# RWKV recurrence: one solve of four tiles against two half chains of two tiles that take turns on TensorE

## The chip, the core and the metric

One NeuronCore of a Trainium2 chip runs the whole program in one launch. The metric is device time in microseconds. The kernel before took 2664.04 us, the median of three runs (2661.07 to 2665.22).

## What is computed

Two layers of a decoder trunk over 256 tokens of width 2048. Layer 0 is latent attention beside a gated delta rule; layer 1 is RWKV-7 time mixing; each is followed by a SwiGLU feed-forward block, and all of it is in float32. The change touches only the RWKV layer:

```
r, k, v = xr @ w_r, xk @ w_k, xv @ w_v          # three 2048 x 2048 projections
def step(state, inp):                            # 32 heads of 64
    r_t, d_t, k_t, v_t, kk_t, a_t = inp
    sk = einsum("bhvk,bhk->bhv", state, kk_t)
    state = state*d_t - sk*(kk_t*a_t) + v_t*k_t
    return state, einsum("bhvk,bhk->bhv", state, r_t)
y = group_norm(y)*ln_w + ln_b + bonus;  return (y * gate) @ w_o
```

The kernel does not walk the tokens. It cuts them into four chunks of 64, inverts one triangular 64x64 matrix per head and chunk, and walks the four chunks.

## The kernel before, in words

**Tiles.** 2048 channels are 16 tiles of 128 partitions, two heads to a tile. Tiles come in 8 pairs. Per pair, `rec_pre` makes r and k: 192 matmuls of 256 columns (lines L317, L319, L320, since every product is done in three parts, high by high, high by low, low by high). `rec_head` makes from them the four matrices `KR`, `AB`, `KG`, `BT` of each tile and the values `V`, with matmuls into the PSUM tag `ph` (L1364, L1374, L1394).

**The solve.** `rec_solve(g)` takes four tiles, and there are four of them, g = 0 to 3. It has three parts:
- *Doubling*: four levels of two steps. A step is one burst `mul` of 64 products of 32x32 (128 matmul instructions, since a float32 product is two passes) at L1413, whose result goes through PSUM to VectorE (`W`, L1427) or to ScalarE and VectorE (`Tm`, L1431, and the transposed `Rc`, L1432), and from there into the next burst. Two smaller bursts (L1439, L1450) end it.
- *Scan*: four chunks. In each, `X` (L1466, L1469), `E` (L1476) and the state `S` (L1488, L1490), each waiting for the one before to come back from PSUM.
- *Output*: for each pair of the four tiles, 88 products (L1509), a sum over the head (`headsum`), the norm, the gate (L1531), and the result goes to DRAM or into `xs_hi`, `xs_lo`.

Each step of a solve needs the result of the step before, so a solve by itself leaves TensorE waiting. The waiting time is meant to be filled by projections: `rec_pre` of later pairs, and in the last two solves `wo_part` (matmuls of 512 columns, L317, L322, L323). I call these two "projections" below, whatever their width.

**Buffers.** `NH` = 5 tiles of `KR`, `AB`, `KG`, `V`, `BT` exist, so that beside the four of a running solve one more can be made; the other three wait for the solve's output. The tag `gt` holds one gate, `BK` one scaled k tile of a head.

**What sets the order.** `weave` emits the tasks by hand-written due times (`LS` is the time given to a solve). A scheduler with a timeline of its own then sets the order of each engine's instructions; on the chip each engine runs its queue in that order. SP issues the loads.

Of the kernel before, what the change touches and what calls it, by code (L numbers as in the profile page):

```python
# [19 lines left out]
P = 128  # L20
# [24 lines left out]
def constants():  # L45
# [32 lines left out]
    out["cent"] = np.tile(np.eye(64) - 1.0 / 64, (2, 1))  # L78
# [25 lines left out]
def tile_trunk(ctx: ExitStack, tc: tile.TileContext, A, out, dbg=None):  # L104
# [1156 lines left out]
    rebank(2, {"ph": 3, "pc": 3})  # L1261
    rcx, rcp = phase("rec")
    RB = {"r_t": 2, "KR": NH, "AB": NH, "KG": NH, "V": NH, "BT": NH, "bon": 3, "pd": 2}
# [13 lines left out]
    def c64(ap):  # L1277
        return ap.rearrange("p (c n) -> p c n", n=64)
# [32 lines left out]
    def rec_head(pr2):  # L1311
# [77 lines left out]
        vb = c64(pbank("ph"))  # L1389
        for j in range(2):  # L1390
            for ch in range(4):
                tsl = slice(ch * 64, ch * 64 + 64)
                for s_ in HS:
                    mm(vb[s_, 4 * j + ch, :], lhsT=vc[s_, j, tsl], rhs=C("cent")[s_], start=True, stop=True)  # L1394
        for j, c in enumerate(cs):
            V = Sr([P, 4, 64], "V")
            act(V, vb[:, 4 * j : 4 * j + 4, :], AF.Copy)
            heads[c] = (*out[j], V)
        heads["pair", pr2] = pd, bon

    def rec_solve(g):
# [3 lines left out]
        U4 = range(4)  # L1405
        UC = [(u, ch) for u in U4 for ch in range(4)]

        def mul(L, X):

            v_ = c32(pbank("pc"))  # L1410
            for u, ch in UC:
                for b, s_ in enumerate(QS):
                    mm(v_[s_, 4 * u + ch, :], lhsT=L(b, u, ch), rhs=X[s_, 4 * u + ch, :], start=True, stop=True)  # L1413
            return v_


        Rw = Sr([P, 16, 64], "R")
        for u in U4:
            tt(Rw[:, 4 * u : 4 * u + 4, :], AB[u][:, :, 0:64], bcn("rm1t", 4), ALU.mult)
        R = Sr([P, 16, 32], "Rc")  # L1420
        tt(R, Rw[:, :, 0:32], Rw[:, :, 32:64], ALU.add)
        Tm = Sr([P, 16, 32], "Tm")
        nc.vector.transpose(flat(Tm), flat(R))
        for lv in (2, 4, 8, 16):
            W = Sr([P, 16, 32], "W")
            p_ = mul(lambda b, u, ch: AB[u][QS[b], ch, 32 * (b % 2) : 32 * (b % 2) + 32], Tm)
            tt(W, p_, bcn(f"rl{lv}", 16), ALU.mult)  # L1427
            yield 1
            p_ = mul(lambda b, u, ch: R[QS[b], 4 * u + ch, :], W)
            Tm, R = Sr([P, 16, 32], "Tm"), Sr([P, 16, 32], "Rc")  # L1430
            act(flat(Tm), flat(p_), AF.Copy)  # L1431
            nc.vector.transpose(flat(R), flat(p_))  # L1432
            yield 1

        Rc, R = R, Sr([P, 16, 64], "R")
        p_ = c32(pbank("pc"))
        for u, ch in UC:
            for b in (0, 2):
                mm(p_[QS[b + 1], 4 * u + ch, :], lhsT=AB[u][QS[b], ch, 32:64], rhs=Tm[QS[b], 4 * u + ch, :],  # L1439
                   start=True, stop=True)  # L1440
        W = Sr([P, 16, 32], "W")
        act(W[QS[1]], p_[QS[1]], AF.Copy)
        nc.vector.tensor_copy(W[QS[3]], p_[QS[3]])
        tt(R.rearrange("p c (b n) -> p c b n", b=2), Rc.unsqueeze(2).to_broadcast([P, 16, 2, 32]),
           C("bd32").rearrange("p (b n) -> p b n", b=2).unsqueeze(1).to_broadcast([P, 16, 2, 32]), ALU.mult)
        yield 1
        p_ = c32(pbank("pc"))
        for u, ch in UC:
            for b in (0, 2):
                mm(p_[QS[b], 4 * u + ch, :], lhsT=W[QS[b + 1], 4 * u + ch, :], rhs=Rc[QS[b + 1], 4 * u + ch, :],  # L1450
                   start=True, stop=True)
        act(R[QS[0], :, 32:64], p_[QS[0]], AF.Copy)
        nc.vector.tensor_copy(R[QS[2], :, 32:64], p_[QS[2]])
        yield 1

        Ss = Sr([P, 3, 4, 64], "S")
        E2 = [Sr([P, 2, 4, 64], t) for t in ("Tm", "Rc")]

        def E(ch):
            return E2[ch // 2][:, ch % 2]  # L1460

        for ch in range(4):
            px = c64(pbank("pc")[:, :T])
            for u in U4:
                for s_ in HS:
                    mm(px[s_, u, :], lhsT=KG[u][s_, ch, 0:64], rhs=V[u][s_, ch, :], start=True, stop=ch == 0)  # L1466
                if ch:
                    for s_ in HS:
                        mm(px[s_, u, :], lhsT=KR[u][s_, ch, 0:64], rhs=Ss[s_, ch - 1, u, :], start=False, stop=True)  # L1469
            X = Sr([P, 4, 64], "X")  # L1470
            act(X, px, AF.Copy)
            yield 1
            pe = c64(pbank("pc")[:, :T])
            for u in U4:
                for s_ in HS:
                    mm(pe[s_, u, :], lhsT=R[s_, 4 * u + ch, :], rhs=X[s_, u, :], start=True, stop=True)  # L1476
            nc.vector.tensor_copy(E(ch), pe)
            if ch in (1, 2):
                dec = Sr([P, 4, 64], "X")
                for u in range(2):  # L1480
                    tt(dec[:, 2 * u : 2 * u + 2, :], Ss[:, ch - 1, 2 * u : 2 * u + 2, :],
                       pds[u][:, :, ch].unsqueeze(2).to_broadcast([P, 2, 64]), ALU.mult)
            yield 1
            if ch < 3:
                pS = c64(pbank("pc")[:, :T])
                for u in U4:
                    for s_ in HS:
                        mm(pS[s_, u, :], lhsT=BT[u][s_, ch, 1, :], rhs=V[u][s_, ch, :], start=True, stop=False)  # L1488
                    for s_ in HS:
                        mm(pS[s_, u, :], lhsT=BT[u][s_, ch, 0, :], rhs=E(ch)[s_, u, :], start=False, stop=True)  # L1490
                if ch:
                    tt(Ss[:, ch], dec, pS, ALU.add)
                else:
                    nc.vector.tensor_copy(Ss[:, 0], pS)
                yield 1
        for v in range(2):
            pr2 = 2 * g + v
            py = pbank("pc")
            y4 = py.rearrange("p (u c n) -> p u c n", u=2, n=64)
            for w_ in range(2):  # L1500
                u = 2 * v + w_
                for i in range(3):
                    for ch in range(4):
                        if i == 1 and ch == 0:
                            continue
                        for s_ in HS:
                            lhs, rhs = ((V[u][s_, ch, :], KG), (Ss[s_, max(ch - 1, 0), u, :], KR),
                                        (E(ch)[s_, u, :], AB))[i]
                            mm(y4[s_, w_, ch, :], lhsT=lhs, rhs=rhs[u][s_, ch, 64:128], start=i + ch == 0, stop=i == 2,  # L1509
                               skip_group_check=True)  # L1510
            yield 1
            sq = Sr([P, 2, T], "W")
            act(flat(sq), py, AF.Square)
            pv = pbank("pc")
            hl = Sr([P, 2, 2 * T], "R", F32R)
            headsum(pv, flat(sq), hl[:, 0, :], hl[:, 1, :])
# [128 lines left out]
```

## Time and profile before

| | us |
|---|---|
| median of three runs | 2664.04 |
| the profiled execution | 2662.39 |
| its span | 2660.6 |
| PE busy in the span | 2569.1 (97%) |
| DVE busy | 1540.4 (58%) |
| ACT busy | 1315.0 (49%) |

The RWKV recurrence stands between 1395 and 1908 us. "Busy" counts a matmul from its start to its modelled end, and those overlap, so a busy PE need not be at its peak: in the solves the number of matmuls in a stretch tells more than the share. PEclk in the tables is the granted clock of TensorE; 1.00 is its upper level of 2.4 GHz, 0.50 its lower one of 1.2 GHz.

### The profile page before, as it was taken

The numbers are of one execution on the slowest core, as the hardware profiler recorded it, in microseconds if no ns is written. First come the engines' busy times: TensorE is split into PE (matmuls) and PEld (weight loads), VectorE is DVE, ScalarE is ACT, GpSimd is POOL, SyncE is SP. The second block draws the span as 40 slices with busy tenths as digits, with TensorE's granted clock in tenths as the row PEclk, the third lists the DMA queues.
The fourth block names the chain that finished last, engine by engine and source line by source line (L and its number), as shares of the span: only waits on it lengthen the run. The fifth ranks groups of instructions, "written<-read, shape, count | busy, mean of one in ns | idle before, by whom it ended". The sixth has DMA issues, their size and how long they took to land.

```text
span 2660.6 us, 50321 instructions
## 1 busy us (share of the span) xinstructions
PE 2569.1 (97%) x21102; PEld 2225.8 (84%) x21102; DVE 1540.4 (58%) x2183; ACT 1315.0 (49%) x1953; POOL 33.3 (1%) x99
## 2 busy tenths in 40 slices
PE   8999999999999999998999998889899999999998
PEld 8999988788888888887999897777688888888886
DVE  7866666655444554458776574664655444555455
ACT  6665545544444434445577473553554444443443
POOL 1000000000000000000000000000000000000000
PEclk9999999999999999998999998899899999999999
DMA  7544546666566656655587442533366666666665
GB/s 208 148 121 129 175 144 198 179 185 194 183 192 187 193 187 190 190 186 176 177 278 219 130 133 67 171 99 126 112 185 190 190 192 193 187 193 194 190 184 164
DMA packets 275331, 461.49 MB, mean 173 GB/s; under 512 B 23752, under 2 KB 89216, under 8 KB 274336
## 3 DMA queue, kind: packets, MB, share of 16 engines
q1 hardware_dynamic: 274720, 458.12, 56.6%
q8 instruction: 165, 2.70, 0.4%
q14 instruction: 62, 0.51, 0.1%
q0 software_dynamic: 384, 0.16, 0.0%
HBM read 441.93 MB, written 16.29 MB: 172 GB/s over the span
## 4 chain that ended last, share of the span: by engine, by line
PE 92%; DVE 3%; ACT 2%; DMA 2%; issue 1%; SPq 0%; DVEq 0%; ACTq 0%
PE pw L317 27%; PE pw L322 20%; PE pw L323 20%; PE pw L320 7%; PE pw L319 7%; PE pc L1413 2%; PE ph L1364 1%; PE pc L1509 1%; DVE wlo L274 1%; DMA raw<-in_rwkv_w_o_dram 1%; PE pc L1476 1%; ACT whi L273 1%; PE pw L1176 1%; PE pc L1490 0%; PE pc L1469 0%
## 5 line engine op out<-in xcount | busy, mean ns | idle before, releaser
L274 DVE TENSOR_TENSOR wlo<-raw,whi 128x1024 fp32r<-128x1024 f32 (+1 forms) x814 | 975.9, 1201 | 881.1 <-ACT whi L273 877.4
L273 ACT ACTIVATE whi<-raw 128x1024 fp32r<-128x1024 f32 (+1 forms) x814 | 844.4, 1040 | 971.3 <-PE pw L323 795.9
L322 PE MATMUL pw<-wlo,xs_hi 128*128 128x512 f32 x1664 | 651.9, 392 | 0.0
L323 PE MATMUL pw<-whi,xs_lo 128*128 128x512 f32 x1664 | 648.8, 391 | 0.0
L317 PE MATMUL pw<-whi,xs_hi 128*128 128x512 f32 x1664 | 599.6, 393 | 0.7 <-ACT fw L465 0.7
L322 PEld LDWEIGHTS pw<-wlo,xs_hi 128*128 128x128 f32 x1664 | 313.6, 188 | 65.0 <-issue 0.7
L317 PEld LDWEIGHTS pw<-whi,xs_hi 128*128 128x128 f32 x1664 | 313.1, 188 | 65.5 <-issue 1.0
L323 PEld LDWEIGHTS pw<-whi,xs_lo 128*128 128x128 f32 x1664 | 313.2, 188 | 65.3 <-issue 0.7
L317 PE MATMUL pw<-xs_hi,whi 128*128 128x256 f32 x1168 | 334.1, 288 | 4.2 <-ACT xs_hi L1148 3.6
L319 PE MATMUL pw<-xs_lo,whi 128*128 128x256 f32 x1168 | 332.5, 286 | 0.0
L320 PE MATMUL pw<-xs_hi,wlo 128*128 128x256 f32 x1168 | 329.7, 287 | 0.3 <-DVE wlo L274 0.3
L323 PE MATMUL pw<-whi,hidl 128*128 128x512 f32 x704 | 276.7, 393 | 0.0
L322 PE MATMUL pw<-wlo,hidh 128*128 128x512 f32 x704 | 275.9, 392 | 0.0
L317 PE MATMUL pw<-whi,hidh 128*128 128x512 f32 x704 | 250.2, 393 | 0.0
L317 PEld LDWEIGHTS pw<-xs_hi,whi 128*128 128x128 f32 x1168 | 224.1, 192 | 6.0 <-ACT xs_hi L1148 3.9
L319 PEld LDWEIGHTS pw<-xs_lo,whi 128*128 128x128 f32 x1168 | 224.0, 192 | 0.9 <-DVE xs_lo L1138 0.3
L320 PEld LDWEIGHTS pw<-xs_hi,wlo 128*128 128x128 f32 x1168 | 221.9, 192 | 1.2 <-DVE wlo L274 0.5
L323 PEld LDWEIGHTS pw<-whi,hidl 128*128 128x128 f32 x704 | 132.3, 188 | 30.0
L317 PEld LDWEIGHTS pw<-whi,hidh 128*128 128x128 f32 x704 | 132.3, 188 | 29.3
L322 PEld LDWEIGHTS pw<-wlo,hidh 128*128 128x128 f32 x704 | 132.3, 188 | 29.0
L320 PE MATMUL pw<-xr_hi,wlo 128*128 128x256 f32 x288 | 82.1, 285 | 2.4 <-DVE wlo L274 2.3
L317 PE MATMUL pw<-xr_hi,whi 128*128 128x256 f32 x288 | 82.1, 285 | 2.0 <-ACT whi L273 2.0
(582 smaller groups left out, 2502.0 us busy)
## 6 DMA issues: line engine op xcount, KB each, us to landing
raw<-in_ffn_w_gate_dram SPq DMA_DIRECT2D x176, 512.0 KB, 3.8
raw<-in_ffn_w_up_dram SPq DMA_DIRECT2D x176, 512.0 KB, 3.7
raw<-in_ffn_w_down_dram SPq DMA_DIRECT2D x176, 512.0 KB, 3.7
raw<-in_hyb_w_in_dram SPq DMA_DIRECT2D x80, 512.0 KB, 3.7
raw<-in_hyb_w_out_dram SPq DMA_DIRECT2D x32, 512.0 KB, 3.9
raw<-in_rwkv_w_v_dram SPq DMA_DIRECT2D x32, 512.0 KB, 4.4
raw<-in_rwkv_w_r_dram SPq DMA_DIRECT2D x32, 512.0 KB, 4.5
raw<-in_rwkv_w_k_dram SPq DMA_DIRECT2D x32, 512.0 KB, 4.2
```

The costliest lines, as they stand in the source:

```text
L273: behind(act(hi, src, AF.Copy), after[0])
L274: behind(tt(lo, src, hi.bitcast(F32), ALU.subtract), after[1])
L317: mm(dst, lhsT=lh, rhs=rh, start=start, stop=False, skip_group_check=True)
L319: mm(dst, lhsT=lh, rhs=rl, start=False, stop=False, skip_group_check=True)
L320: mm(dst, lhsT=ll, rhs=rh, start=False, stop=stop, skip_group_check=True)
L322: mm(dst, lhsT=lh, rhs=rl, start=False, stop=False, skip_group_check=True)
L323: mm(dst, lhsT=ll, rhs=rh, start=False, stop=stop, skip_group_check=True)
L1176: mm(ps[:96, 0, :], lhsT=wt[:, (c + j) % 8, :], rhs=xm[:, j, :], start=c + j == 0, stop=c + j == ND - 1)
L1364: mm(g[:, ch * P : (ch + 1) * P], lhsT=bdk[:, ch, i, :], rhs=KR[:, ch, :], start=True, stop=True)
L1413: mm(v_[s_, 4 * u + ch, :], lhsT=L(b, u, ch), rhs=X[s_, 4 * u + ch, :], start=True, stop=True)
L1476: mm(pe[s_, u, :], lhsT=R[s_, 4 * u + ch, :], rhs=X[s_, u, :], start=True, stop=True)
L1509: mm(y4[s_, w_, ch, :], lhsT=lhs, rhs=rhs[u][s_, ch, 64:128], start=i + ch == 0, stop=i == 2, skip_group_check=True)
```

## The change

`rec_solve` becomes two chains of two tiles, `chain(0)` and `chain(1)`, that are emitted step by step in turn. All their tiles and PSUM banks are doubled in number and halved in size. A burst is now 32 products (64 matmul instructions), and `cm` puts every matmul behind the other chain's burst before it, by an order only, without a semaphore. The outputs take turns too, and work in halves of 256 columns. `V` comes from two full-array products per tile in place of eight of 64x64, and is copied from PSUM by ScalarE and VectorE in four parts. The gate takes the buffer of `BK`, and `k_t` gets a second buffer. In the scheduler, heads get a lead of 1500 and solves of 4000 ahead of the projections.

```
-    rebank(2, {"ph": 3, "pc": 3})
+    rebank(2, {"ph": 2, "pc0": 2, "pc1": 2})
-    RB = {"r_t": 2, "KR": NH, ...
+    RB = {"k_t": 2, "r_t": 2, "KR": NH, ...
...
-            for ch in range(4):
-                for s_ in HS:
-                    mm(vb[s_, 4 * j + ch, :], lhsT=vc[s_, j, tsl], rhs=C("cent")[s_], start=True, stop=True)
+            for b in range(2):
+                mm(vb[:, (2 * j + b) * P : (2 * j + b + 1) * P], lhsT=vc[:, j, b * P : (b + 1) * P], rhs=C("cent"),
+                   start=True, stop=True)
...
+        def burst():
+            order["last"] = order["now"]
+        def cm(*a, **k):
+            order["now"] = behind(mm(*a, **k), order["last"])
+        def chain(v):
+            UC = [(u, ch) for u in range(2) for ch in range(4)]
...
+                v_ = c32(pbank(pc)[:, :T])
+                burst()
+                for u, ch in UC:
+                    for b, s_ in enumerate(QS):
+                        cm(v_[s_, 4 * u + ch, :], lhsT=L(b, u, ch), rhs=X[s_, 4 * u + ch, :], start=True, stop=True)
...
+        for f in (chain, output):
+            for _ in zip(f(0), f(1)):
+                yield 1
...
-        gate[pr2] = Sr([P, 2, T], "gt")
+        gate[pr2] = Sr([P, 2, T], "BK")
...
-    LS = 1.5
+    LS = 1.3
-        tasks.append((q - 0.5, q + 0.45, 10, rec_head(q)))
+        tasks.append((q - 0.5, q + 0.45, 10, rec_head(q), 1500))
-        tasks.append((t, t + LS, 28, rec_solve(g)))
+        tasks.append((t, t + LS, 28, rec_solve(g), 4000))
```

What it does to the order, at three places. In the rows, `pc` is the solve's PSUM tile (the two chains have different numbers), `ph` the heads', `pw` the projections'.

PE, the doubling of the first solve, before: one step and the start of what follows it.

```order
L1364 MATMUL ph_15043<-KR_14869,bdk 128x128 x4
L1364 MATMUL ph_15049<-KR_14869,bdk 128x128
L1413 MATMUL pc_14551<-Tm_14527,AB_13694 32x32 x16
L1413 MATMUL pc_14551<-Tm_14527,AB_13812 32x32 x16
L1413 MATMUL pc_14551<-Tm_14527,AB_14091 32x32 x16
L1413 MATMUL pc_14551<-Tm_14527,AB_14209 32x32 x16
L1364 MATMUL ph_15049<-KR_14869,bdk 128x128 x3
L317 MATMUL pw_14325<-xr_hi,whi_14882 128x256
```

Behind the last of these rows stand 18 projection matmuls before the next burst, and some 18 to 26 between any two bursts of this doubling. After, at the same place:

```order
L1422 MATMUL pc_14714<-Tm_14660,AB_13694 32x32 x16
L1422 MATMUL pc_14714<-Tm_14660,AB_13812 32x32 x16
L1422 MATMUL pc_14749<-Tm_14697,AB_14085 32x32 x16
L1422 MATMUL pc_14749<-Tm_14697,AB_14203 32x32 x16
L1374 MATMUL ph_15222<-cst_77,BC_14964 128x128 x2
L1422 MATMUL pc_14806<-W_14713,Rc_14661 32x32 x32
L1422 MATMUL pc_14843<-W_14748,Rc_14698 32x32 x32
L1422 MATMUL pc_14887<-Tm_14839,AB_13694 32x32 x16
L1422 MATMUL pc_14887<-Tm_14839,AB_13812 32x32 x16
```

The bursts of the two chains follow each other, and no projection stands between them; from the fifth of the eight steps at the latest all four doublings are like that.

PE, the scan of the first solve, second chunk, before:

```order
L1476 MATMUL pc_15331<-X_15323,R_15089 64x64 x8
L1488 MATMUL pc_15366<-V_13916,BT_13752 64x64 x2
L1466 MATMUL pc_15432<-V_13916,KG_13695 64x64 x2
L1490 MATMUL pc_15366<-Tm_15191,BT_13752 64x64 x2
L1488 MATMUL pc_15366<-V_13918,BT_13860 64x64 x2
L1490 MATMUL pc_15366<-Tm_15191,BT_13860 64x64 x2
```

The scan stands alone, without a projection. After, from the same solve's scan:

```order
L320 MATMUL pw_15570<-xr_hi,wlo_15573 128x256
L317 MATMUL pw_15183<-xs_hi,whi_15479 128x256
L319 MATMUL pw_15183<-xs_lo,whi_15479 128x256
L320 MATMUL pw_15183<-xs_hi,wlo_15480 128x256
...
L319 MATMUL pw_15570<-xr_lo,whi_15572 128x256
L1422 MATMUL pc_15306<-S_15202,KR_13658 64x64 x2
L1422 MATMUL pc_15306<-V_13909,KG_13813 64x64 x2
L1422 MATMUL pc_15306<-S_15202,KR_13782 64x64 x2
L1422 MATMUL pc_15317<-V_14295,KG_14086 64x64 x2
```

Twelve projection matmuls now stand ahead of the matmuls that wait for the new state `S`; 3 to 22 stand at such places, in the scans of g = 0 and 2 throughout, in g = 1 in the first half only, in g = 3 nowhere.

DVE, the end of the third solve's output and the next head, after:

```order
L1560 TENSOR_TENSOR W_19425<-W_19425,Tm_19426 128x256
L274 TENSOR_TENSOR xs_lo<-yg_20603,xs_hi 128x512
L1562 TENSOR_TENSOR bon_17944<-W_19425,bon_17944 128x256
L1563 TENSOR_TENSOR bon_17944<-bon_17944,BK_19132 128x512
L1351 TENSOR_TENSOR BK_19500<-kh_19456,ip_18792 128x4x64
L1352 TENSOR_TENSOR BK_19500<-r_19462,pis_19442 128x4x64
L1351 TENSOR_TENSOR BK_19606<-kh_19456,ip_18792 128x4x64
```

The gate (L1563) now reads a `BK` buffer, and the next head's `BK` stands right behind it.

## Rows read from the trace of the kernel before

**Rows 1.** Doubling and scan of each solve: length, busy (count) by engine, PEclk, DMA.

```profile
1472.10:1516.20 44.10, 42.86 (x1393) 40.24 (x1392) 25.49 (x34) 20.97 (x34) 1.22 (x2) 1.00 0.43 131
1516.20:1547.30 31.10, 26.20 (x543) 23.02 (x538) 15.97 (x32) 13.39 (x26) 1.46 (x6) 1.00 0.22 67
1579.80:1625.50 45.70, 38.82 (x1347) 36.32 (x1346) 21.16 (x27) 18.19 (x31) 0.82 (x2) 0.89 0.42 126
1625.50:1656.30 30.80, 26.83 (x506) 23.54 (x506) 13.58 (x30) 10.29 (x23) 1.46 (x6) 0.83 0.07 19
1689.70:1731.40 41.70, 31.43 (x1254) 27.84 (x1253) 17.74 (x25) 15.71 (x30) 0.82 (x2) 0.79 0.40 133
1731.40:1763.80 32.40, 28.39 (x506) 24.28 (x506) 15.97 (x32) 11.76 (x24) 1.66 (x6) 0.84 0.13 38
1795.40:1848.70 53.30, 51.11 (x1325) 41.31 (x1324) 29.33 (x33) 20.75 (x25) 0.00 (x0) 1.00 0.44 140
1848.70:1884.20 35.50, 24.70 (x438) 21.51 (x437) 10.46 (x21) 7.66 (x15) 0.00 (x0) 0.67 0.12 37
```

**Rows 2.** The same stretches and three more, of projections (`pw`) alone: first count is PE's.

```profile
1472.10:1516.20 44.10, 27.58 (x214) 25.68 (x214) 0.00 (x0) 0.58 (x1) 1.00 0.43 131
1516.20:1547.30 31.10, 5.39 (x39) 4.69 (x39) 0.00 (x0) 1.08 (x2) 1.00 0.22 67
1579.80:1625.50 45.70, 20.41 (x160) 18.98 (x159) 0.00 (x0) 0.00 (x0) 0.89 0.42 126
1625.50:1656.30 30.80, 2.61 (x17) 2.37 (x17) 0.00 (x0) 1.09 (x2) 0.83 0.07 19
1689.70:1731.40 41.70, 11.00 (x67) 9.09 (x66) 0.00 (x0) 0.00 (x0) 0.79 0.40 133
1731.40:1763.80 32.40, 4.31 (x17) 3.03 (x17) 0.00 (x0) 0.60 (x1) 0.84 0.13 38
1795.40:1848.70 53.30, 38.10 (x157) 28.60 (x156) 5.41 (x8) 2.35 (x4) 1.00 0.44 140
1848.70:1884.20 35.50, 0.00 (x0) 0.34 (x1) 0.00 (x0) 0.00 (x0) 0.67 0.12 37
1446.50:1456.50 10.00, 10.00 (x86) 10.00 (x86) 0.00 (x0) 0.58 (x1) 1.00 0.70 203
1884.20:1888.60 4.40, 4.38 (x11) 3.46 (x11) 0.00 (x0) 0.00 (x0) 0.53 0.03 10
1888.60:1893.00 4.40, 4.40 (x21) 3.62 (x21) 0.00 (x0) 0.00 (x0) 1.00 0.31 89
```

**Rows 3.** Timeline of PE in doublings: start, length, line, count, idle before and releaser.

```profile
1615.87 1.39 PE L1413 MATMUL pc<-W,Rc 32*32 32x32 f32 x87 [2.30 <-issue]
1620.16 0.85 PE L1439 MATMUL pc<-Tm,AB 32*32 32x32 f32 x23 [0.81 <-issue]
...
1711.35 1.04 PE L1413 MATMUL pc<-Tm,AB 32*32 32x32 f32 x100 [0.50 <-issue]
1713.18 0.44 PE L1413 MATMUL pc<-W,Rc 32*32 32x32 f32 x28 [0.79 <-DVE W L1427]
1715.10 1.59 PE L1413 MATMUL pc<-W,Rc 32*32 32x32 f32 x100 [1.47 <-issue]
```

**Rows 4.** DMA queue of instructions between 1709 and 1727: packets, MB, share.

```profile
q8 instruction: 5, 0.08, 2.1%
```

**Rows 5.** Timeline of PE in the first solve's scan, one chunk's three waits.

```profile
1525.44 0.68 PE L1476 MATMUL pc<-X,R 64*64 64x64 f32 x16 [0.54 <-ACT X L1471]
...
1526.65 0.33 PE L1490 MATMUL pc<-Tm,BT 64*64 64x64 f32 x4 [0.29 <-DVE Tm L1477]
...
1528.20 0.33 PE L1469 MATMUL pc<-S,KR 64*64 64x64 f32 x4 [0.52 <-DVE S L1492]
...
1529.77 0.68 PE L1476 MATMUL pc<-X,R 64*64 64x64 f32 x16 [0.53 <-ACT X L1471]
```

**Rows 6.** The values' matmuls in the groups of PE: count, busy us, mean ns.

```profile
L1394 PE MATMUL ph<-cst,v_t 64*64 64x64 f32 x256 | 9.2, 221 | 0.0
```

**Rows 7.** The gate's load in the DMA issues: count, KB each, us to landing.

```profile
gt<-gts SPq DMA_DIRECT2D x8, 256.0 KB, 4.0
```

More of the change, by code (lines that the diff above doesn't have):

```diff
@@ L77, in constants @@
     out["bd32"] = (i[:, None] % 64 // 32 == q[None, :] // 32) * 1.0
-    out["cent"] = np.tile(np.eye(64) - 1.0 / 64, (2, 1))
+    out["cent"] = np.kron(np.eye(2), np.eye(64) - 1.0 / 64)
     out["bd64"] = (i[:, None] // 64 == i[None, :] // 64) * 1.0
@@ L1404, in rec_solve @@
         pds, bons = zip(*(heads.pop(("pair", 2 * g + u)) for u in range(2)))
[L1405 to L1410, printed above, removed]
-            for u, ch in UC:
[L1412 to L1419, printed above, removed]
@@ L1435, in rec_solve @@
[L1435 to L1445, printed above, removed]
@@ L1446, in rec_solve @@
[L1446 to L1467, printed above, removed]
-                    for s_ in HS:
[L1469 to L1479, printed above, removed]
-                for u in range(2):
[L1481 to L1486, printed above, removed]
-                    for s_ in HS:
[L1488 to L1494, printed above, removed]
-                yield 1
@@ L1496, in rec_solve @@
-        for v in range(2):
-            pr2 = 2 * g + v
-            py = pbank("pc")
+        R, Ss, E = [None, None], [None, None], [None, None]
+        Rw = [Sr([P, 8, 64], f"R{v}") for v in range(2)]
+        for u in range(4):
+            last = tt(Rw[u // 2][:, 4 * (u % 2) : 4 * (u % 2) + 4, :], AB[u][:, :, 0:64], bcn("rm1t", 4), ALU.mult)
+        order = {"last": None, "now": None}
+        def burst():
+            order["last"] = order["now"]
+        def cm(*a, **k):
+            order["now"] = behind(mm(*a, **k), order["last"])
@@ L1499, in rec_solve, with output, Sv @@
+        def output(v):
+            pr2 = 2 * g + v
+            pc = f"pc{v}"
+            def Sv(shape, tag, dt=F32):
+                return Sr(shape, tag + str(v), dt)
+            py = pbank(pc)
+            burst()
             y4 = py.rearrange("p (u c n) -> p u c n", u=2, n=64)
@@ L1519, in rec_solve @@
-            act(sq, r0, AF.Square)
+            bon = flat(bons[v])
+            pv = pbank(pc)
+            qs = []
+            for j in range(2):
+                sl = slice(j * T, (j + 1) * T)
+                sq = Sv([P, T], "W")
+                act(sq, py[:, sl], AF.Square)
+                headsum(pv[:, sl], sq, Sv([P, T], "Tm", F32R), Sv([P, T], "Rc", F32R))
             yield 1
-            stt(sq, pv, 64 * 64e-5, sq, ALU.add, ALU.mult)
-            act(sq, sq, AF.Copy, scale=-0.5 / 64, bias=1.5)
```

125 lines of the change are left out of this document (93 added, 32 removed).

## The prediction

> **What bounds the kernel now.** TensorE: it is busy for 97% of the span, so only the places where it waits can give anything, and the change touches only the four solves. I read two tables of them first, the stretches as a whole and the projections in them. The reader is to see that TensorE's time in a solve has two parts, projections, which have to be done anyway somewhere, and the rest, which I call the **net time** of the solve: length less projections. A projection matmul of 256 columns takes 10.0 / 86 = 0.116 us at the full clock, one of 512 columns 4.4 / 21, some 0.22 us with the overlap at the edges [rows 2]. The solves last 75.2, 76.5, 74.1 and 88.8 us [rows 1]. Their projections are 253 and 177 narrow ones, then 48 narrow and 36 wide, then 157 wide ones [rows 2] (the third solve's two widths are counted in its order): 29.3, 20.5, 13.5 and 34.5 us. The net times are 45.9, 56.0, 60.6 and 54.3 us, 216.8 in sum. That is what the change can shorten; the projections only move.
>
> Then the timeline, to see what the net time waits for. There are two different things.
>
> In the **scan** TensorE waits for the chain: 0.54 us for `X`, 0.29 for `E`, 0.52 for `S`, in a chunk that takes 1529.77 - 1525.44 = 4.33 us [rows 5]. No projection stands there, 39, 17, 17 and 0 in the four scans with their outputs [rows 2], and the clock falls to 0.83, 0.84 and 0.67 in the last three [rows 1].
>
> In the **doubling** it waits for its own instructions. After 28 matmuls of a burst it stops for 1.47 us with nothing to wait for ("issue"), and the places where it starts again are 1715.10 - 1711.35 = 3.75 us and 100 + 28 = 128 matmuls apart; earlier 1620.16 - 1615.87 = 4.29 us for 87 + 41 [rows 3] (the 41 stand between the two rows). A matmul comes with its weight load, so 128 of them are 256 instructions, and the instruction queue brought 5 packets of 16 KB in that stretch of 18 us, one in 3.6 us [rows 4]. 256 instructions of 64 bytes are one such packet. I read it so: TensorE fetches its program one packet ahead, a fetch takes 3.6 us when the DMA queues are quiet and 4.3 or more when weights are loading, and a packet whose matmuls run faster than that makes it wait. The four doublings have 1393, 1347, 1254 and 1325 matmuls, 41.6 packets: at 3.6 us that is 150 us of their 184.8 us [rows 1], and most of the other 35 are packets full of projections that last longer than their fetch. So the doubling before is already as fast as its instructions arrive, and projections in it cost little.
>
> The Trainium skill has a rule against this reading: Runtime: NRT & Kernel Launch, "Instruction fetch mechanics", tells of the same 16 KiB blocks of 256 instructions, but calls the cost of crossing a block mostly hidden, as instructions are issued more slowly than they are filled in. The 1.47 us pause [rows 3] differs from that; its outcome is the last rival.
>
> **The change part by part.**
>
> *Half chains, doubling.* The work is the same: twice as many bursts of half the size. What each chain waits for is covered by the other's burst, 64 matmuls, half of the 128 that a burst has now: the wait for `W` is 0.79 us [rows 3] and shrinks with the halved width. But the instructions are not fewer, and the order puts the bursts behind each other without projections. By the program's order the doublings now have 1275, 1230, 1213 and 1202 matmuls, 38.4 packets, and in them 102 and 49 narrow and 32 and 42 wide projections. At 3.6 us a packet that is 138 us; counted packet by packet, with those that are thick with projections at their own length, 148.5. Less the projections (17.5 + 16.3 us), the net time is **114.7 us**. Before, the same stretches hold 422 narrow and 176 wide ones (49.0 + 38.7 us), net 184.8 - 87.7 = 97.1 us. So the doublings lose 17.6 us by the change, since 373 of their 598 projections leave them.
>
> *Half chains, scan and output.* Before, net: 26.6, 28.8, 28.7 and 35.5 us, 119.6 in all. In the first scan, which ran at the full clock, the three waits are 1.35 us a chunk, some 5 us over the four chunks [rows 5], and the drain of each burst about 1 more; with 3 to 22 projections (0.3 to 2.5 us) ahead of every dependent burst these are covered. I take 20 us for g = 0 and 2 (21 with nothing else won, 18.6 at best), 23 for g = 1, where the second half has no projections and only the other chain's burst as a cover, and 27 for g = 3, without projections and with the tail of two outputs at the end; between 22 (full clock throughout) and 35.5 (nothing won). Sum **90 us**.
>
> *The clock.* A doubling that waits for packets lets the clock fall, as it did in the second and third (0.89 and 0.79, while the first, filled, kept 1.00) [rows 1]. All four are now of that kind. The projections of the scan bring it back: after the last solve 11 wide ones took 4.4 us, then 21 in the next 4.4 [rows 2], so one return costs about 4.4 - 11 x 0.22 = 2 us; three of them, **6 us** (the fourth is inside the 27).
>
> *Values on the full array.* The 256 passes of L1394 are busy 9.2 us in all [rows 6] and become 64 of four times the area; the gain lies between nothing and 9.2 us; I take 1.5, as the new ones are no cheaper one by one than a narrow projection of 0.116 us. The four smaller copies of `V` lie beside projections.
>
> *Gate in `BK`, heads, `k_t`.* A gate's load lands after 4.0 us [rows 7], and the second gate of a solve can only be issued when the first has been used; the next head's `BK` stands behind it on VectorE, and on SP the weight loads behind the gate's. Between the first three solves 166 and 145 projection matmuls stand in a row (19 and 17 us), which hide it. Ahead of the fourth solve only some 10 us of projections stand against the chain of output, gate, two heads; cost 0 to 8 us, I take 2. The second `k_t` only lets `rec_pre` run ahead. The wider copies on VectorE and ScalarE (two of 256 columns for one of 512) cost overhead beside a TensorE that waits for packets.
>
> **Sum.** 114.7 + 90 + 6 = 210.7 against 216.8: -6.1; -1.5 for the values, +2 ahead of the fourth solve: -5.6 us. From the profiled execution's 2662.4 that is **2657 us**; that execution is 1.6 us below the median of 2664.0, which is within the runs' spread.
>
> **The rivals.**
>
> *The packets take longer (slower than before).* One mechanism, in the doublings: when weights load, a packet took 4.29 us [rows 3]. At 4.25 us the same packet count gives 169 us in place of 148.5, so +20: **2677 us**. It decides from about 3.75 us a packet on, where the gain is gone. For it: gates, heads' inputs and weights still load at each doubling's start. Against: with the projections standing still the three weight buffers fill and the queues go quiet, as in the 18 us that gave 3.6.
>
> *The scans win less (no change).* If the clock stays low in the scans, as in the last one now (0.67), half a scan at half the clock costs some 5 us in each of two: **2662 us**. Against: the projections in them.
>
> *Packets do not bind.* The pauses could come from something that goes with the long bursts. Then the doubling would go by its bursts, 8 steps of two halves at some 1.3 us (28 matmuls in 0.44 us and 100 in 1.04, less the overlap [rows 3]), 10.4 us, with some 6.6 for the two small bursts, the heads and what is left of the waits, 17 us net a solve: 68 in place of 114.7, **2610 us**. Against it stands the even spacing of 128 matmuls. The rule of the Trainium skill named above would have it come out like this.
>
> **How the numbers follow.** Forecast 0.42, packets longer 0.27, scans win less 0.24, packets not binding 0.07. A run can tell about 0.2% (5.3 us) from no change, and the forecast lies at that edge: of its 0.42 I count 0.09 as no change, of the second rival 0.21, the rest 0.03 as slower. Faster 0.40, same 0.30, slower 0.30. The range goes from 2640 (packets at 3.5 us and the scans at their best) to 2680 (4.25 us and the costlier scans), and leaves out the last rival and the far end of the first.
>
> **What would show it.** Right: in the doublings of the changed kernel pauses on "issue" every 128 matmuls, 3.5 to 3.8 us apart, with the clock at its lower level; scans of g = 0 and 2 with projections and hardly any wait; 36 to 40 us for each doubling. Wrong: doublings under 30 us, or a packet well over 4 us; waits on ScalarE or VectorE ahead of most bursts of the scan; a long wait ahead of the fourth solve.

## The result, and the profile after

The changed kernel took 2698.01 us, the median of four runs (2697.31 to 2699.71), against 2663.65 us for the kernel before beside it: ratio 1.0131, 95% interval 1.0113 to 1.0148. It is 34 us slower, where 2657 us and a small gain were forecast.

The profiled execution has a span of 2696.3 us, 35.7 more than before. The page's first part (busy us, share of the span, instructions):

```profile
PE 2581.7 (96%) x20926; PEld 2235.1 (83%) x20926; DVE 1564.6 (58%) x2335; ACT 1330.6 (49%) x2049; POOL 38.6 (1%) x99
```

The shares tell nothing of the loss, so the stretches have to be read. First the projections of each stretch, as in [rows 2]: start and end, length, busy (count) of PE, weight loads, DVE and ACT, then PEclk, DMA share, GB/s. For each of the four solves the rows are doubling, scan with output, and the interval to the next solve; the fourth has no interval.

```profile
1473.40:1515.50 42.10, 15.84 (x102) 14.46 (x102) 0.00 (x0) 0.57 (x1) 0.84 0.30 91
1515.50:1556.40 40.90, 23.24 (x169) 20.64 (x169) 0.00 (x0) 1.18 (x2) 0.98 0.36 111
1556.40:1604.10 47.70, 39.69 (x306) 38.04 (x306) 0.00 (x0) 1.75 (x3) 0.94 0.53 166
1604.10:1644.80 40.70, 7.68 (x50) 6.66 (x49) 0.00 (x0) 0.00 (x0) 0.71 0.19 56
1644.80:1676.30 31.50, 12.95 (x93) 11.53 (x93) 0.00 (x0) 1.08 (x2) 1.00 0.36 111
1676.30:1717.40 41.10, 32.12 (x220) 28.55 (x220) 0.00 (x0) 1.16 (x2) 1.00 0.62 212
1717.40:1760.50 43.10, 9.57 (x33) 5.69 (x32) 0.00 (x0) 1.09 (x2) 0.76 0.25 77
1760.50:1815.00 54.50, 32.58 (x132) 24.08 (x132) 0.00 (x0) 3.58 (x6) 0.96 0.39 126
1815.00:1850.10 35.10, 13.85 (x48) 9.83 (x48) 1.45 (x3) 0.00 (x0) 0.81 0.26 83
1850.10:1892.80 42.70, 13.20 (x42) 9.12 (x42) 2.59 (x4) 0.00 (x0) 0.68 0.16 53
1892.80:1921.20 28.40, 1.66 (x6) 1.05 (x6) 1.38 (x2) 0.00 (x0) 0.92 0.12 39
```

And the three intervals of the kernel before, which [rows 2] do not have:

```profile
1547.30:1579.80 32.50, 27.00 (x215) 26.20 (x215) 0.00 (x0) 1.18 (x2) 1.00 0.57 177
1656.30:1689.70 33.40, 27.88 (x223) 27.12 (x223) 0.00 (x0) 1.17 (x2) 1.00 0.61 193
1763.80:1795.40 31.60, 23.74 (x98) 18.00 (x98) 0.00 (x0) 2.25 (x4) 1.00 0.54 165
```

With the prediction's prices (0.116 us for a narrow projection, 0.22 for a wide one; the first five rows are narrow, the 220 are 192 narrow and 28 wide, from 1717 on all are wide) the net times are:

| net us | before | forecast | after |
|---|---|---|---|
| four doublings | 97.1 | 114.7 | 134.5 |
| four scans with output | 119.6 | 90 + 6 | 94.6 |
| three intervals | 25.1 | 25.6 | 49.3 |
| sum | 241.8 | 236.3 | 278.4 |

In sum the scans came out as forecast. The doublings are 20 us worse than forecast, the intervals 24 us. The 36.6 us between the sums are the whole loss; the forecast had -5.5.

One thing moved besides the projections: the matmuls of the heads (`ph`), which this net time counts as a stretch's own. Of them alone, the first scan and the first interval, before and then after:

```profile
1516.20:1547.30 31.10, 4.92 (x55) 3.75 (x55) 2.65 (x4) 2.65 (x7) 1.00 0.22 67
1547.30:1579.80 32.50, 7.29 (x74) 6.16 (x74) 4.08 (x6) 3.92 (x11) 1.00 0.57 177
```

```profile
1515.50:1556.40 40.90, 0.12 (x1) 0.12 (x1) 0.00 (x0) 0.00 (x0) 0.98 0.36 111
1556.40:1604.10 47.70, 12.48 (x71) 10.34 (x71) 6.65 (x12) 5.62 (x17) 0.94 0.53 166
```

The second and third solve show the same: 55 head matmuls in the scan before, 1 after. At what they take from start to start at the full clock (0.112 us for 128 columns, 0.22 for 512, 0.03 for the small ones of the values) some 12 us of heads left the three scans, of which 8 went to the intervals and 4 to the doublings. Heads apart, the scans gained 13 us and not 25, and the intervals lost 16 us and not 24, 12 of the 16 ahead of the fourth solve.

Next, the doubling's pauses: PE in the fourth doubling (start, length, count, idle before and its releaser), and the DMA of the 20 us around them (busy share in tenths and GB/s in 40 slices of 0.5 us, then the queue).

```profile
1863.55 1.76 PE L1422 MATMUL pc<-W,Rc 32*32 32x32 f32 x116 [3.36 <-issue]
...
1867.31 1.77 PE L1422 MATMUL pc<-Tm,AB 32*32 32x32 f32 x116 [1.83 <-issue]
...
1871.05 1.76 PE L1422 MATMUL pc<-W,Rc 32*32 32x32 f32 x116 [1.81 <-issue]
...
1874.52 1.76 PE L1422 MATMUL pc<-Tm,AB 32*32 32x32 f32 x116 [1.54 <-issue]
...
1877.99 1.72 PE L1422 MATMUL pc<-W,Rc 32*32 32x32 f32 x113 [1.54 <-issue]
```

```profile
DMA  0000010000001000000010000001000000100000
GB/s 0 0 0 0 0 33 0 0 0 0 0 0 33 0 0 0 0 0 0 0 33 0 0 0 0 0 0 33 0 0 0 0 0 0 33 0 0 0 0 0
q8 instruction: 5, 0.08, 1.6%
```

This is [rows 3] and [rows 4] over again, with nothing else around it. TensorE runs 1.8 us and, after the first row, stands 1.5 to 1.8 us, in turns of 3.47 to 3.76 us; the 12 to 15 matmuls that complete a turn's 128 stand between the rows. In each turn one 16 KB packet arrives, on queues that do nothing else. A packet arrives in one slice, and six or seven slices are empty before the next: what counts is the time from one packet to the next, not the bandwidth, 33 GB/s in one slice of seven or eight and nothing in the others. Over all four doublings of the changed kernel, two pauses on issue in a row stand 128 or 256 matmuls apart, whatever burst that falls in. The 14 turns of 128 took 3.47 us (eight), 3.75 (five) and 4.02, 3.61 on average.

Last, the wait that costs most, ahead of the fourth solve. PE's waits from 1815 to 1850 (in total, times, longest), then DVE's two products with the gate in the third solve, first of the kernel before, then of the changed one:

```profile
PE pw L317 <- ACT xs_hi L273: 9.8, 2, 8.9
```

```profile
1768.62 0.69 DVE L1531 TENSOR_TENSOR bon<-bon,gt 128x512 f32<-128x512 f32 x1
...
1788.18 0.69 DVE L1531 TENSOR_TENSOR bon<-bon,gt 128x512 f32<-128x512 f32 x1
```

```profile
1825.22 0.68 DVE L1563 TENSOR_TENSOR bon<-bon,BK 128x512 f32<-128x512 f32 x1
...
1832.46 0.69 DVE L1563 TENSOR_TENSOR bon<-bon,BK 128x512 f32<-128x512 f32 x1
1833.18 0.42 DVE L1351 TENSOR_TENSOR BK<-kh,ip 128x256 f32<-128x256 f32 x1
```

Before, the first pair's product with the gate began 1768.6 - 1763.8 = 4.8 us after the last output matmul. After, the two outputs share VectorE and ScalarE and it began 1825.2 - 1815.0 = 10.2 us after it. The result goes through DRAM to `xs_hi`, for which the next projections wait 8.9 us. The next head's `BK` waits for the second gate, which sits in its buffer until 1832.5 + 0.7 us. In this solve neither product waited for the gate's load; in the first solve the second one waited 2.5 us for it:

```profile
1585.44 0.69 DVE L1563 TENSOR_TENSOR bon<-bon,BK 128x512 f32<-128x512 f32 x1 [2.51 <-DMA BK<-gts]
```

### The profile page after: what moved, and what is told of

Read it like the earlier page. It is cut to its first block, busy times and chain, and to the rows that moved or that the text cites. A ratio compares the mean times of both kernels' runs of the same rounds, so it can differ in the third digit from the quotient of the medians.

```text
span 2696.3 us, 50334 instructions
## 1 busy us (share of the span) xinstructions
PE 2581.7 (96%) x20926; PEld 2235.1 (83%) x20926; DVE 1564.6 (58%) x2335; ACT 1330.6 (49%) x2049; POOL 38.6 (1%) x99
## 4 chain that ended last, share of the span: by engine, by line
PE 89%; DVE 4%; DMA 3%; ACT 2%; issue 2%; SPq 0%; DVEq 0%; ACTq 0%
PE pw L317 26%; PE pw L323 20%; PE pw L322 20%; PE pw L320 6%; PE pw L319 6%; PE pc L1422 4%; DVE wlo L274 1%; PE ph L1364 1%; ACT whi L273 1%; PE pw L1176 1%; DMA Pt<-pts 1%; DMA raw<-in_rwkv_w_r_dram 0%; PE pA L521 0%; PE pB L521 0%; DMA yg<-ygs 0%
```

## The experiments

All ratios are to the kernel before, in runs on the same chip. 0.001 is 2.7 us.

**Is the doubling bound by packets?** Three kernels take instructions out of it. The first two do it with the same result: the two diagonal 32x32 blocks of a half head become one 64x64 product, with masked weights.

```
+            AD[:, 4*u : 4*u+4, :] = ab[u][:, :, 0:64] * bd32
-                p_ = mul(lambda b, u, ch: ab[u][QS[b], ch, 32 * (b % 2) : 32 * (b % 2) + 32], Tm)
+                for u, ch in UC:
+                    for s_ in HS:
+                        cm(p_[s_, 4 * u + ch, :], lhsT=AD[s_, 4 * u + ch, :], rhs=Tm[s_, 4 * u + ch, :], ...)
```

On the changed kernel:

> The changed kernel with the first product of each level in blocks of 64x64 (lhsT masked to its two diagonal blocks) in place of 32x32: the same result, 256 matmuls fewer in each doubling (two packets of 128). Theory A (the doubling goes by its packets, at 4.1 us each): the four doublings fall from 168.5 to some 135 us, the projections in them nearly the same in sum, so 25 to 30 us less than the changed kernel, ratio 1.001 to 1.004. Rival D (the doubling goes by the turns of the two chains, their round trips over VectorE and ScalarE): bursts as many and as far apart, 0 to 5 us less, ratio 1.011 to 1.013.

Measured 1.0086 (1.0064 to 1.0107): 12 us less than the changed kernel, between the two. The groups of PE in the second doubling show why, first of the changed kernel, then of this one (count, busy, mean ns, idle before by releaser); then, from this one's timeline, a burst of each form at the full clock:

```profile
L1422 PE MATMUL pc<-Tm,AB 32*32 32x32 f32 x576 | 9.4, 221 | 5.3 <-issue 3.9 <-ACT Tm L1454 1.4
L1422 PE MATMUL pc<-W,Rc 32*32 32x32 f32 x512 | 7.3, 215 | 4.6 <-issue 4.6
```

```profile
L1422 PE MATMUL pc<-Tm,R 64*64 64x32 f32 x256 | 12.0, 256 | 3.5 <-ACT Tm L1461 3.2 <-issue 0.2
L1422 PE MATMUL pc<-W,Rc 32*32 32x32 f32 x512 | 7.2, 218 | 1.3 <-issue 0.6 <-DVE W L1457 0.5
```

```profile
1477.59 1.31 PE L1422 MATMUL pc<-W,Rc 32*32 32x32 f32 x128
...
1480.90 2.06 PE L1422 MATMUL pc<-Tm,R 64*64 64x32 f32 x64 [1.57 <-ACT Tm L1461]
```

The pauses on issue all but vanish: 8.5 us to 0.8 in this doubling, 35 to 3 over the four (summed from the timeline's rows, here and below). So they do go by the number of instructions, and rival D is out. But half as many matmuls of 64x32 took longer than the small ones: 64 of them 2.06 us, 128 of 32x32 only 1.31. TensorE was busy 16 us more in the four doublings (142 us for 126), which ate half the gain, and 5 us more went into waits on ScalarE and VectorE.

> The kernel before with the same edit: first product of each level in blocks of 64x64, 256 matmuls fewer in each doubling, the order of everything else the same. Theory A: at 4.1 us a packet, packets thick with projections at their own length, the four doublings fall from 184.8 to some 165 us: 17 us less, ratio 0.993 to 0.995. Rival D (each burst waits for the chain): the wait for W and Tm stays, 0 to 4 us less, ratio 0.9985 to 1.000.

Measured 0.9986 (0.9969 to 1.0002), 4 us less, no more than rival D said, and the interval reaches no change. Here the pauses were only 13 us to begin with; they fell to 5, and TensorE was busy 7 us more. The edit does not help. Theory A's 17 us was wrong: it left out the longer matmuls and took more from the pauses than they held.

The third leaves two levels out (`for lv in (2, 4)` for `(2, 4, 8, 16)`), so that the matmuls stay as they are:

> The changed kernel without the levels 8 and 16 of the doubling, so that part of the inverse is left out: 512 matmuls fewer in each doubling, 10 bursts of each chain become 6. Theory A2 (packets of 128 matmuls, 3.75 us each, decide there): 4 packets or 15 us less in each solve, the pauses on issue in the doublings fall from 35 to 15 us or less, 45 to 60 us less than the changed kernel, ratio 0.991 to 0.997. Rival E (the small matmuls' own time decides, 65.6 us for the 4608 of them, 14 ns each): 7.3 us a solve, 29 us less, ratio 1.001 to 1.004.

Measured 0.9941 (0.9926 to 0.9956): 51 us less than the changed kernel. The doublings are 26.2, 25.8, 30.3 and 25.3 us, 61 less in sum; 4 packets of 3.75 us in each would be 60, of 3.6 us 58. Pauses on issue: 16 us. The engine's own time would have given 29. The edit also takes 4 of the 10 steps of each chain away, so by itself it cannot tell packets from round trips (four tenths of 168.6 us would be 67). The changed kernel's trace can: its doublings hold 35 us of pauses on issue and 7 us of waits on ScalarE and VectorE. **Shown, by these kernels and the turns of 128 matmuls together: a bare doubling, one with hardly a projection in it, is as long as its packets take to arrive.**

**Does what stands in a doubling cost anything?** Six idle matmuls of 256 columns ahead of each large burst of the changed kernel:

```
+                for _ in range(6):
+                    cm(bk[:, T:], lhsT=bd64r, rhs=xs_hi[:, 15, :], start=True, stop=True, ...)
```

> The changed kernel with six idle matmuls of 256 columns (into the unused half of the burst's bank) ahead of each of the sixteen larger bursts of a solve: 96 a solve, 0.116 us each, 44.5 us of work that the result does not need. The order takes 119 narrow and 29 wide projections (20 us) out of the doublings for them. Theory A2 (a doubling lasts about 38 to 45 us whatever fills it): the doublings grow by 8 us or less in sum, and the total by what was pushed out, 18 to 28 us more than the changed kernel, ratio 1.020 to 1.024. Rival E (the engine's own time decides): the whole 44 us, ratio 1.029 to 1.031.

Measured 1.0204 (1.0186 to 1.0223): 19 us more for 44.5 us of work, as theory A2 has it. The doublings were 39.2, 40.1, 43.3 and 40.0 us, 6 less in sum than without the idle matmuls, though these are 11 us in each; 20 us of projections made room for them. The granted clock in the doublings was 1.00, 0.91, 0.96 and 1.00, where the changed kernel had 0.84, 0.71, 0.76 and 0.68. Eight doublings of several kernels show a slow growth too; the projections are priced as above:

| doubling of | projections in it, us | length, us |
|---|---|---|
| h2_undo2, second | 0 | 35.0 |
| e2_nolead, second | 0 | 38.2 |
| changed kernel, second | 5.8 | 40.7 |
| before, third | 9.5 | 41.7 |
| changed kernel, first | 11.8 | 42.1 |
| g1_dblhalf, fourth | 18.5 | 42.9 |
| before, first | 24.8 | 44.1 |
| before, fourth | 34.5 | 53.3 |

From nothing to 25 us of projections these grow by 6 to 9 us. They are chosen rows, and not all fit: the first of h1_undo3 took 51.0 us with 12 us in it, the second of h4_undo4 47.2 with 10, the fourth of f6_values 59.0 with 32. Over all 56 doublings of the fourteen kernels that have every small matmul and no idle one, the best straight line through lengths against projections is 39 us and 0.4 us for each us of projections, with a scatter of some 3 us. So a projection that leaves a doubling gives back about 0.4 of its time there, and the rest is paid elsewhere.

**Which part of the change costs what?** One part at a time on the kernel before, or undone on the changed one. Only the scan as two half chains (`for _ in zip(half(0), half(1))` around the loop over `ch`, with `px`, `pe`, `pS`, `X` and `S` of two tiles):

> The kernel before with only the scan as two half chains (PSUM two banks for the heads and four for the solve); doubling, output, values, gate and leads as before. Theory A2 (the changed kernel loses in the doublings, where its bursts stand without projections at TensorE's lower clock, and in the intervals that took the heads out of the scans; its scans do win): doublings as before within 3 us, the four scans 10 to 20 us shorter, ratio to before 0.992 to 0.996. Rival F (the half scans win nothing of their own; what looked like their gain is the heads that left them for the intervals): ratio 0.998 to 1.002.

Measured 0.9921 (0.9906 to 0.9936), **2641.43 us: it beats both kernels**. Its four scans to the last output matmul, projections alone as above:

```profile
1522.90:1551.00 28.10, 6.78 (x50) 6.16 (x50) 0.00 (x0) 1.08 (x2) 1.00 0.27 84
...
1627.60:1653.40 25.80, 3.39 (x25) 3.16 (x25) 0.00 (x0) 1.08 (x2) 0.91 0.12 36
...
1729.70:1756.90 27.20, 4.65 (x19) 3.38 (x19) 0.00 (x0) 0.60 (x1) 0.91 0.16 40
...
1838.70:1858.60 19.90, 0.00 (x0) 0.00 (x0) 0.00 (x0) 0.00 (x0) 0.91 0.09 30
```

Each is 3 to 10 us shorter than in [rows 2] (the fourth would be 29.9 there to the same point), though it holds as many projections or more. TensorE waits 4 us in the four where it waited 20, with the heads still in them (55 head matmuls in each of the first three, as before), so rival F is out. The doublings lost some of it: to their last small matmul they took 189.6 us for 183.3, 3 us more than the expectation allowed.

Only the doubling as two half chains, on the kernel before:

> The kernel before with only the doubling as two half chains (scan, output, values, gate and leads as before; two banks for the heads, four for the solve). Its doublings hold 98, 44 and 61 narrow and 18 and 84 wide projections in place of 214, 159 and 48 narrow and 18 and 156 wide; the scans hold more. Theory A2 (a doubling lasts 38 to 45 us whatever stands in it up to some 25 us of projections, so projections that leave it are paid elsewhere): the doublings fall only from 183 to about 169 us while 41 us of projections leave them, of which the scans' waits hide some 24; 2 to 10 us more than before, ratio 1.000 to 1.004. Rival H (half chains hide the round trips, so the doubling wins outright): ratio 0.985 to 0.995.

Measured 1.0014 (1.0001 to 1.0027), 4 us more. The doublings are 40.8, 36.9, 42.2 and 42.9 us, 20 less than before to the same point, but 41 us of projections left them. The half chains do hide round trips: the waits on ScalarE and VectorE in the doublings fall from 6 us to 3. But there was little to hide, and the pauses on issue rise from 13 us to 29.

Only the gate in the buffer of `BK`:

> The kernel before with only the gate in the buffer of the heads' scaled k tile. Heads and the next solve come later in the order: the doublings hold 214 and 82 narrow, then 6 and 96 wide projections, and the intervals 292, 278 and 165 in place of 215, 223 and 36 to 97. Theory A2: some 30 us of projections leave the doublings, which shorten by half of that, and the chain of output, gate and heads waits as in the changed kernel: 10 to 20 us more, ratio 1.004 to 1.0075. Rival I (the shared buffer costs only a wait of its own, hidden by the projections ahead of the heads): 0 to 6 us more, ratio 1.000 to 1.002.

Measured 1.0061 (1.0037 to 1.0084), 16 us more. Projections of the first interval and the second doubling, where [rows 2] and the interval above had 215 and 160:

```profile
1552.90:1594.20 41.30, 35.98 (x292) 35.21 (x292) 0.00 (x0) 1.15 (x2) 1.00 0.63 191
1594.20:1633.60 39.40, 10.55 (x83) 9.66 (x82) 0.00 (x0) 0.00 (x0) 0.82 0.31 91
```

The heads and with them the solve come later, the projections run ahead of it in the interval, and the doubling that had use for them is bare. The wait itself is small; the order costs: net, by the same prices, its doublings take 19 us more, its scans 4, its intervals 2. Undone on the changed kernel (own buffer, `k_t` single):

> The changed kernel with the gate back in a buffer of its own (and k_t with one buffer, so that it fits). Theory A (the loss is packets in the doublings, some 20 us more than forecast, and the chain of output, gate, heads ahead of the fourth solve, some 15 us more than forecast; the shared buffer is what makes that chain long): the 8.9 us wait ahead of the fourth solve goes, 10 to 15 us less than the changed kernel, ratio to before 1.007 to 1.009. Rival B (the chain is long because the output's norm and gate in halves are slow on VectorE and ScalarE, and the solve's heads come behind it whatever buffer the gate has): within 4 us of the changed kernel, ratio 1.011 to 1.015.

Measured 1.0088 (1.0066 to 1.011), 11 us less, as theory A has it. The 8.9 us wait is gone (2.4 us is now the longest in that interval), but the fourth doubling is 6 us longer. The outputs are no earlier for it: the first product with the gate begins 8.4 us after the last output matmul (10.2 in the changed kernel), the second 33.9 us after it (17.4).

Only the values:

> The kernel before with only the values on the full array and their copies in four parts. The step of the prediction: 1.5 us less, between 0 and 9.2; ratio 0.997 to 1.000. Rival (the four copies and the order that they change lengthen the heads, ahead of the fourth solve above all): 1.001 to 1.004.

Measured 1.0047 (1.0032 to 1.0062), 12.5 us more, above even the rival. Again the order moved: the first two intervals hold 28 and 19 narrow projections more than before, the second and third doubling 41 and 25 fewer, and the doublings' net time rose from 97 to 113 us. Why the fourth takes 59.0 us with 12 wide projections fewer than before is not found; it has two pauses on issue of 2.9 and 2.6 us.

The turns and the leads, undone on the changed kernel (`mm` in place of `behind(mm, last)`; no 1500 and 4000):

> The changed kernel without the order of the turns (the half chains may overlap as the scheduler likes); its doublings then hold 122 and 112 narrow and 91 and 49 wide projections in place of 102, 49, 32 and 42. Theory A2 (projections in the doublings run in the pauses and keep the clock up): 8 to 18 us less than the changed kernel, ratio 1.006 to 1.010. Rival G (the turns are what keeps the chains from waiting for each other): what the projections win the waits of the chains take, ratio 1.012 to 1.016.

> The changed kernel without the leads of 1500 and 4000. Rival C (the leads are what takes the projections out of the doublings and starves the intervals): the time falls by 17 us or more, ratio 1.007 or less, with projections between the bursts again. Theory A: the order shows as few projections in the doublings without the leads (98, 0, 20 and 25) as with them, so nothing comes back; within 6 us of the changed kernel, ratio 1.011 to 1.015, doublings 36 to 42 us.

Without turns 1.0092 (1.0075 to 1.0109), 10 us less: the doublings hold 58 us of projections in place of 34 and the pauses on issue fall from 35 to 18 us. Without leads 1.0152 (1.0134 to 1.0171), 6 us more, in an interval that overlaps the changed kernel's; rival C is out. On the half scans alone the leads change nothing:

> The kernel before with the half scans (as f1_scanhalf) and the leads of 1500 for heads and 4000 for solves with LS of 1.3 untouched at 1.5. The doublings hold about as much as in f1_scanhalf (204, 156, 60 narrow, 18 and 144 wide), the scans more (77 and 36 narrow, 30 wide). Theory A2: the same as f1_scanhalf within 5 us, ratio 0.990 to 0.994. Rival C (the leads cost by themselves): ratio 0.996 or more.

Measured 0.9916 (0.9888 to 0.9943), as theory A2 has it.

**Do the parts add up?** Three and then two parts undone together:

> The changed kernel with three parts undone together: gate in its own buffer (k_t single), values as before, no order of turns. Left of the change are the half chains in doubling, scan and output and the leads. The doublings hold 103, 95, 58 narrow and 18 and 73 wide projections. Theory A2 (a doubling's length goes by its packets and its projections, the half scans win what f1_scanhalf won): doublings about 169 us, 50 us of it projections, net 119 against 104 in f1_scanhalf, scans 4 us better: 9 to 15 us above f1_scanhalf, so below the kernel before, ratio 0.994 to 0.998. Rival J (the half outputs, or what else is left, lose by themselves): ratio 1.002 or more.

> The same with the order of the turns kept, so only gate and values are undone. The doublings hold 17 and 0 narrow, 58 narrow and 18 wide, and 2 wide projections: nearly bare. Theory A2: doublings about 155 us with 13 us of projections in them, net 142: 20 to 26 us more than h1_undo3, ratio 1.002 to 1.007. Rival K (bare doublings are short, so that nothing is lost by turns): within 6 us of h1_undo3.

Measured 1.0063 (1.0043 to 1.0083) and 1.0096 (1.0076 to 1.0115). The first expectation failed, on the side of rival J: from the parts it should have been below 1. The second kernel took 9 us more than the first, nearer to rival K's 6 than to the 20 to 26 of theory A2: it has nearly bare doublings of 39.2, 35.0, 41.2 and 38.3 us, as short as expected (153.7 in sum), but h1_undo3's were 190 with 50 us of projections in them, not 169. So something else in h1_undo3 lost. Two more kernels looked for it:

> The kernel before with both the doubling and the scan as half chains, everything else as before (output whole, gate, values, no turns, no leads). The order is that of g1_dblhalf almost row by row, with the scan halved. Theory L (the half chains together need no more than their parts: half scans win on top of half doublings what is left of the scans' waits, 10 to 20 us): ratio 0.993 to 0.998; then the 45 us between f1_scanhalf and h1_undo3 lie in the half outputs and the leads. Theory M (doubling and scan share one cover: the projections that the half doublings push out have no wait left in half scans): no better than g1_dblhalf or worse, ratio 1.001 to 1.007.

> h1_undo3 without the leads too, so that half chains in doubling, scan and output are what is left of the change. Its doublings hold 53, 83, 86 narrow and 18 and 60 wide projections, 43 us, with the scans' 346 narrow and 96 wide. Theory L: the leads cost some of the 45 us, 15 us or more less than h1_undo3, ratio 1.000 or less. Theory M: leads change little with half chains as e2_nolead showed for the whole change, within 8 us of h1_undo3, ratio 1.003 to 1.009.

h3_both: 0.9966 (0.9948 to 0.9984). The half scan wins 13 us on top of g1_dblhalf, as theory L has it; the two share no cover, and theory M is out. h4_undo4: 1.0046 (1.0027 to 1.0066). The leads make 5 us here, which the two intervals do not tell from nothing, so theory L was wrong on them. Between the two kernels lie the half outputs, the banks split by chain and the due times (`LS` of 1.3 for 1.5), 21 us. The gates in the first solve, of h3_both, then of h4_undo4 (both have the gate in its own buffer):

```profile
1564.52 0.68 DVE L1553 TENSOR_TENSOR bon<-bon,gt 128x512 f32<-128x512 f32 x1
...
1587.63 0.68 DVE L1553 TENSOR_TENSOR bon<-bon,gt 128x512 f32<-128x512 f32 x1
```

```profile
1582.70 0.68 DVE L1559 TENSOR_TENSOR bon<-bon,gt 128x512 f32<-128x512 f32 x1
...
1588.14 0.69 DVE L1559 TENSOR_TENSOR bon<-bon,gt 128x512 f32<-128x512 f32 x1 [1.24 <-DMA gt<-gts]
```

The last output matmul ended at 1560.3 and 1553.4. So the whole outputs deliver the pairs after 4.2 and 27 us, the half ones after 29 and 35: in turns, the first pair comes as late as the second. Yet the intervals of h4_undo4 are no longer (89.1 us in sum, 88.9 in h3_both). That the late first pair costs the 21 us is not shown, and which of the three moves the rest of the order is not separated.

As a staircase, each step with one more part (ratio, us to the kernel before):

| kernel | ratio | us |
|---|---|---|
| half scan alone (f1_scanhalf) | 0.9921 | -21 |
| with half doubling (h3_both) | 0.9966 | -9 |
| with half outputs, split banks, `LS` 1.3 (h4_undo4) | 1.0046 | +12 |
| with leads (h1_undo3) | 1.0063 | +17 |
| with turns (h2_undo2) | 1.0096 | +26 |
| with values, gate in `BK`, second `k_t`: the changed kernel | 1.0131 | +35 |

Leads and turns are steps whose intervals overlap; f4_noturn shows the turns' 10 us by itself. The second `k_t` and `LS` were never tried alone.

## Why the prediction was wrong

**What bounds the kernel: right.** The packets of 128 matmuls come 3.47 to 4.02 us apart, 3.61 on average, where the prediction read 3.6 from [rows 3] and [rows 4], and the experiments above show that they set the length of a bare doubling. The rule of the Trainium skill (Runtime: NRT & Kernel Launch, "Instruction fetch mechanics"), by which crossing a block is mostly hidden, does not hold in these bursts: the pauses of 1.5 to 1.8 us above are not hidden, and the rival that it would bear out (2610 us) is out.

**Doublings, forecast 148.5 us, measured 168.6: the failed term.** In the prediction's terms, 54 us of projections leave the doublings, and these were to shorten by 36 us (184.8 to 148.5). They shortened by 16. The count of packets was right, and so was their price. What failed is the price of what else stood in them: the projections and heads were put in at their full-clock durations. The text itself said that the clock would fall in all four, and charged that only for the scans' return. The granted clock was 0.84, 0.71, 0.76 and 0.68. From start to start a narrow projection then took 0.149 us, a wide one 0.297, a head's matmul 0.17 and a small one 0.013, against 0.116, 0.22, 0.112 and 0.010 at the full clock. With these in the same packet count the sum is some 164 us at 3.6 us a packet. So by this count some 15 of the 20 us go with the low clock. It is a count: no run changes the clock alone. g4_dummy goes the same way, with a higher clock, more work and shorter doublings. The last 5 us stay open; the 7 us of waits on ScalarE and VectorE are not in the count.

**Scans, forecast 90 + 6: the number right (94.6), in part by luck.** The working took only waits off the scans' net time and nothing for the heads. But the heads left the scans, some 12 us, and without the heads the scans gained 13 us where 24 were forecast. That half scans can win as much as forecast, heads in place, f1_scanhalf shows: 115.1 us net before, 87.9 after, to the last output matmul. The other parts of the change are not needed for it.

**Gate, heads: forecast 2 us (bounds 0 to 8), measured 24 in the intervals: the other failed term.** Some 8 of the 24 are the heads' own matmuls that came out of the scans, which the prediction did not count. Most of the rest is ahead of the fourth solve, 24.5 us net for 10.0, with the wait of 8.9 us: a long wait there was one of the prediction's signs of being wrong. It put the outputs' work on VectorE and ScalarE at nothing, and the first pair's product with the gate began 10.2 us after the last output matmul in place of 4.8. But that alone does not make the wait: in e1_gt, with the gate in its own buffer, it begins 8.4 us after and no wait over 2.4 us follows. So the wait takes the shared buffer and the order that comes of it. And that 166 and 145 projections hide the rest was true in TensorE's row of waits, but these projections are not free cover: they are the ones the doublings needed. That is what g2_gate shows, 16 us for a buffer, with the loss in the doublings and hardly any in the intervals.

**Values, forecast -1.5: wrong by sign** when made alone (+12.5), by the order again. In the changed kernel it is worth nothing that these runs can tell: e1_gt with the new values has 1.0088, h2_undo2 with the old ones 1.0096.

**The rivals.** "Packets take longer" gave 2677 us and 20 us more in the doublings. That size was right and its mechanism wrong: no turn of 128 matmuls between two pauses took 4.25 us. "Scans win less" did not happen by its mechanism: the granted clock in the scans was 0.98, 1.00, 0.96 and 0.92. No rival had doublings that stay long because what is left in them runs at the low clock, nor heads that move from the scans to the intervals.

## What to carry to other kernels

Where a stretch is bound by something that a filler does not slow (here instruction packets), the filler in it is cheap: on average 0.4 us for each us of projections here. So count what a change moves out of such a stretch at its full price in the place where it lands. Take the length of what stays behind from stretches that are already as bare, at the clock that they are granted, and not from durations at the full clock. A net time that holds several kinds of work can come out right because one of them went elsewhere, so count each kind by itself. A change of several parts is best tried part by part: one of them (the half scan) won 21 us by itself, and with all the rest the kernel lost 35.

## What was not expected of the hardware

A 64x32 product (64 rows, 64 columns of weights, 32 columns moving) took 32 ns from start to start at the full clock (2.06 us for 64), three times a 32x32 one (1.31 us for 128). Two small products were cheaper for the array than the one larger product that took their place, and dearer only in instructions. And while TensorE works through bursts of small matmuls, its instructions come in one packet in some 3.6 us over queues that are empty for some 3 us in between, though the engine stands still for 1.5 to 1.8 us of each turn.
